# A hybrid decoder step on one core: one hand-made instruction list from the delta rule to the end

## The chip, the cores and the metric

The kernel runs on one core of a Trainium2 chip. The metric is the device time of one execution in microseconds (us), the median of the runs. Engines run their own queues in order and meet at semaphores: TensorE (PE in the profile; PEld is its weight load), VectorE (DVE), ScalarE (ACT), GpSimd (POOL) and SyncE (SP), which issues the DMAs.

## The reference, cut to what matters

One step of a decoder with two layers, for a prompt of 1024 tokens and 8 samples of one token, all in float32 with a model width of 1024.

```python
# layer A (gated delta rule), 8 heads of 128
proj = rmsnorm(x, norm_g) @ w_in                    # q, k, v, gate, a, beta
q, k, v = split(silu(causal_conv(proj[qkv])))       # then l2norm of q and k
o, s = gated_delta_rule(q, k, v, g, beta, s0)       # chunks, a state per head
h = x + (rmsnorm(o) * silu(gate)) @ w_out
# shared keys and values of 4 heads of 64
k, v = split(rmsnorm(h) @ w_kv); k = rmsnorm(k, k_norm)
# layer B (window of 128, ALiBi, sinks), 16 query heads in 4 groups
q, gate = split(rmsnorm(h) @ w_in); q = rmsnorm(q, q_norm)
o = softmax_with_sink(q k' - slope * dist) v
y = h + (o * silu(gate)) @ w_out
```

The states of the convolution and of the delta rule, and the last 128 keys and values, are outputs too, for the prompt and for the samples.

## The kernel before, in words

**Arithmetic.** Each operand of a large matrix product is split into a high part of the format fp32r and a low rest (`split`, line 79): ScalarE copies the high part, VectorE subtracts. A product is three chains of matmuls, high x high, high x low and low x high, added in one PSUM bank. The tokens are 8 tiles of 128, and a ninth "tile" (NT) for the 8 samples.

**The delta rule and the list.** From line 393 the program does not emit instructions directly. Generators yield operations (`Op`), and a planner, `Order` (line 478), keeps a planned clock for each engine and each piece of memory. It takes the operation that can start first by its plan (`run`, line 566), with a priority number as the tie-break, and emits it; the order so found is fixed for all engines (`tc.manual_schedule`, line 1388). A TensorE operation whose generator is no filler counts as ready `PEM` = 250 ns late, so filler matmuls go ahead of it. Durations come from formulas (`took`, line 442). The planner compares byte ranges inside a tile (`extent`, line 410; `ready`, line 509). `need` and `get` are waits of a generator for a named event or a free buffer, settled while the list is made; the semaphores between engines come from the framework behind it, which follows tiles and buffers.

Filler in this part is the first layer's input projection (`proj_all`, line 738) and, behind it, `out_all` (line 1363), the first 6 heads' share of the output projection (`K1` = 6): their results go through DRAM (`oD`) and come back in the order of tiles 0 to 7, two chains of 18 matmuls of 512 columns per tile. `out_evac` (line 1353) adds the input to it and stores each tile in DRAM (`hD`). The samples' delta rule comes in two batches of 4 heads (`sample_batch`, line 1147), behind head 3 and head 7; it loads 256 KB pieces of the state twice and stores them.

**Seam.** Behind the list the program closes the delta rule's buffers (line 1394) and is plain code from there on, whose order the framework finds. The loop over tiles at line 1407 loads each tile of `hD`, adds the last two heads' share (chains of 6 matmuls; `ohl`, line 1420, is its split operand; for the samples `ohs`, cleared on GpSimd by `zero_r`, line 1281, with 32 matmuls), stores it again, normalizes the rows, transposes them (line 1447) and splits them into `ng`, the operand of layer B.

**Layer B.** For each of 4 head groups `load_qkv` (line 1525) loads six pieces of weights of 256 KB, multiplies them by the norm's gain on GpSimd (line 92) and splits them. `tile_qkv` (line 1565) makes q, k and v of a tile, 24 matmuls of 384 columns into a bank `pj` (2 banks). Then it normalizes q per head, splits it (`qhl`), transposes the two parts (`tq`, line 1592, 4 transposes into bank `chA`), transposes k into the free columns of `pj`, makes scores with the high and low part of the keys (`sps`), the softmax, transposes of the probabilities (`ptp`, line 1645) and the product with the values (`op`, bank `chB`). The three stages of a tile are interleaved with those of its neighbours by `PIPE` (line 49). Gates (`gate_group`, line 1510: 24 matmuls of 384 or 264 columns into bank `ivY`) are put between by a table of positions (`gpos`, line 1673).

**Output projection.** From line 1702: the attention of the samples, which loads the key and value caches (`kc_`, `vc_`), and a projection in three column blocks with weights `wob`, 24 matmuls per tile, then `hD` is added and the result stored.

Of the kernel before, what the change touches and what calls it, by code (L numbers as in the profile page):

```python
# [20 lines left out]
P = 128  # L21
# [19 lines left out]
NY = 3  # L41
# [5 lines left out]
P3O = [0, 1, 2, 3, 8, 4, 5, 6, 7]  # L47

PIPE = [(1, 1), (0, 0), (2, 2)]
GA = 1  # L50
# [6 lines left out]
def hybrid_step(  # L57
# [384 lines left out]
    def took(op):  # L442
# [3 lines left out]
        name = op.f.__name__  # L446
        if op.e == "P":
# [17 lines left out]
        if op.e == "G":  # L465
            if name == "affine_select":
                return 130 + 1.25 * n
            if name == "tensor_tensor":
                return 100 + 2.35 * n
            return 100 + 0.8 * n if name == "memset" else 200 + 5 * n  # L470
# [7 lines left out]
    class Order:  # L478
# [45 lines left out]
        def emit(self, op, t_):  # L524
            c_ = took(op)
            self.at[op.e] = t_ + c_
            if op.e == "D":
                n = 1
                for d_ in (op.k["out"]).shape:
                    n *= d_  # L530
                self.dma = max(self.dma, t_) + n * 4 / 180.0
                end = self.dma + 2000.0
            else:
                end = t_ + c_ + AFTER[op.e]
# [573 lines left out]
    def store_state(h, st):  # L1108
        yield dq.dma_start(out=ssm_prompt[0, 0, h], in_=st)

# [36 lines left out]
    def sample_batch(h0):  # L1147


        B48 = [P, 4, NS]  # L1150
        units = [(hh, hb) for hh in range(4) for hb in range(2)]
# [10 lines left out]
        yield from need(*[("scb", nm, h0 + i) for nm in "qkv" for i in range(4)])  # L1162
        for u in units[:2]:
            yield load(*u)
        qs, ks, vs = (scb[:, i, h0:h0 + 4, :] for i in range(3))
        egs, bts = (smp[:, i, h0:h0 + 4, :] for i in range(2))
        t3 = gd.tile([P, 4, 4, NS], F32, tag="dl", name="t3", bufs=1)
# [5 lines left out]
        yield pm(sps[:, 0:96], ones, flat(t3[:, 0:3]))  # L1173
        sp = gd.tile([P, 4, 4, NS], F32, tag="dl", name="sp", bufs=1)
        yield sq.copy(flat(sp[:, 0:3]), sps[:, 0:96])
        free("gen")
        rs = sm.tile([P, 2, 4, NS], F32, tag="rs", name="rs", bufs=1)
        yield from rsq(vq, flat(rs), flat(sp[:, 0:2]), 64, 1.0, EPS,
# [4 lines left out]
        kq = sm.tile([P, 4, NS, 2], F32, tag="kq", name="kq", bufs=1)  # L1183
# [3 lines left out]
        spk = sm.tile([P, 4, NS, 2], F32, tag="spk", name="spk", bufs=1)  # L1187
        for i, (hh, hb) in enumerate(units):
# [6 lines left out]
            if i + 2 < 8:  # L1195
                yield load(*units[i + 2])
# [11 lines left out]
        yield vq.tensor_copy(st3[:, 0, :, 0:8], kn)  # L1208
        yield vq.tensor_copy(st3[:, 0, :, 8:16], st3[:, 0, :, 0:8].bitcast(F32))
        yield vq.tensor_tensor(out=st3[:, 0, :, 16:24], in0=kn, in1=st3[:, 0, :, 0:8].bitcast(F32), op=ALU.subtract)  # L1210
        yield vq.tensor_copy(st3[:, 1, :, 0:8], de)
        yield vq.tensor_copy(st3[:, 1, :, 16:24], st3[:, 1, :, 0:8].bitcast(F32))
        yield vq.tensor_tensor(out=st3[:, 1, :, 8:16], in0=de, in1=st3[:, 1, :, 0:8].bitcast(F32), op=ALU.subtract)
# [11 lines left out]
        yield pm(sps[:, 0:32], ones, o2.rearrange("p h b -> p (h b)"))  # L1225
        ro = kqn
        yield from rsq(vq, ro.rearrange("p h b -> p (h b)"), sps[:, 0:32], 32, 1.0 / 128.0, EPS,
# [3 lines left out]
        for hb in range(2):  # L1231
# [10 lines left out]
            for hh in range(4):  # L1242
                if hh < 3:
                    yield again(hh + 1)
# [8 lines left out]
        yield from need(*[("z", h0 + i, 2) for i in range(4)])  # L1253
        om = ogm[:, h0:h0 + 4, :]
# [26 lines left out]
    def zero_r(t_, scr):  # L1281
        G.memset(scr, 0.0)
        G.tensor_copy(t_, scr)
# [7 lines left out]
    def out_gains(p3a):  # L1291
# [7 lines left out]
        free("gen")  # L1299

    rawfree = [0] * RB[0]

    def out_loads():
# [3 lines left out]
        todo = [("w", 0, k, ts(0, 512)) for k in range(K1)] + [("o", 0, k) for k in range(0, K1, 3)]  # L1307
        todo += [("w", 1, k, ts(1, 512)) for k in range(K1)]
        for t in range(1, NT):
            todo += [("o", t, k) for k in range(0, K1, 3)]  # L1310
            if t in (2, 3):
                todo += [("w", 2, k, ts(t - 2, 512)) for k in range(K1, KT)]
        pieces = {}

        def feed2():
            yield from need(("split", 2 * len(jobs) - 1))
            for i, it in enumerate(todo):
                if it[0] == "o":
                    t, k = it[1:]
                    if k == 0:  # L1320
                        yield from need(("o", K1 - 1), ("out",))
                        if t >= 2:
                            yield from need(("ot", t - 2))
                        ohx[t] = (p3a[0].tile([P, D], F32, tag="hx", name="hx"),
                                  p3a[0].tile([P, 2, K1, P], F32R, tag="ohl", name="ohl"))
# [27 lines left out]
    def out_evac(t, ci, ps):  # L1353
# [3 lines left out]
        if ci:  # L1357
            yield dq.dma_start(out=hD[ts(t, P), :], in_=hx)
# [4 lines left out]
    def out_all():  # L1363
# [8 lines left out]
        for t in range(NT):  # L1372
# [8 lines left out]

    for i in range(2):
        for gi in range(4):
            mark("e", i, gi)
    for gi in range(3):
        mark("z", 0, gi)
    ET = mybir.EngineType
    with tc.manual_schedule(engines={ET.PE, ET.DVE, ET.Activation, ET.Pool, ET.SP}):
        for pri, gen_ in ((0, chains()), (1, inverses()), (2, prep_all()), (2.5, decays()), (3, values()), (2.2, norms()),
                          (5, conv_all()), (1.2, feed()), (1.2, split_all()), (7, samples()), (FILL, proj_all())):  # L1390
            spawn(pri, gen_)
        od.run()
    wb = wb_[0]
    es2.close()

    es4 = ExitStack()
    ng = []
    for i, (_, gn) in enumerate(GRP):
        npool = es4.enter_context(tc.tile_pool(name=f"npool{i}", reuse_waits="tile", bufs=1))
        ng.append(npool.tile([P, 2, KT, gn], F32R, name=f"ng{i}"))  # L1400
    hs = npool.tile([P, KT, 40], F32R, name="hs")
    with tc.tile_pool(name="p3", reuse_waits="tile", bufs=2) as p3:
        scr = p3.tile([P, KT, 40], F32, tag="scr", name="scr", bufs=1)
        zero_r(hs, scr)
        ohs = p3.tile([P, KT, 40], F32R, tag="ohs", name="ohs", bufs=1)
        zero_r(ohs, scr)
        for t in P3O:
            samp = t == NT
            n = NS if samp else P
            g, off = divmod(t * P, 384)  # L1410
            hx = p3.tile([P, D], F32, tag="hx", name="hx", bufs=4)
            DMA.dma_start(out=hx[:n], in_=x_sample[:, 0, :] if samp else hD[ts(t, P), :])
            if samp:
                S.copy(ohs[:, :, 0:NS], ogm)
                V.tensor_tensor(out=ohs[:, :, 32:32 + NS], in0=ogm, in1=ohs[:, :, 0:NS].bitcast(F32), op=ALU.subtract)
            else:
                ohl = p3.tile([P, 2, KT - K1, P], F32R, tag="ohl", name="ohl2")
                oc = ogs[:, :, ts(t, P)]
                S.copy(ohl[:, 0], oc)
                V.tensor_tensor(out=ohl[:, 1], in0=oc, in1=ohl[:, 0].bitcast(F32), op=ALU.subtract)  # L1420
            for ci in range(2):
                c_ = ts(ci, 512)
                ps = pj.tile([P, 512], F32, tag="pj", name="pj")
                if samp:
                    for b in range(2):
                        for k in range(KT):
                            w_ = wa[ci][:, b, k, :] if k < K1 else wb[:, b, k - K1, c_]
                            mm(ps[:40], ohs[:, k, :], w_, b + k == 0, b + k == KT)
                else:
                    for i, (a, b) in enumerate(PRS):  # L1430
                        for k in range(KT - K1):
                            mm(ps, ohl[:, a, k, :], wb[:, b, k, c_], i + k == 0, i == 2 and k == KT - K1 - 1)
                V.tensor_tensor(out=hx[:n, c_], in0=hx[:n, c_], in1=ps[:n], op=ALU.add)
                if samp:
                    V.tensor_tensor(out=hx[:n, c_], in0=hx[:n, c_], in1=ps[32:32 + n], op=ALU.add)
            DMA.dma_start(out=hD[t * P:t * P + n, :], in_=hx[:n])
            hn = p3.tile([P, D], F32, tag="hn", name="hn", bufs=3)
            ss = sm.tile([P, 1], F32, tag="ss", name="ss")
            r = sm.tile([P, 1], F32, tag="r1", name="r1")
            S.activation(hn[:n], hx[:n], AF.Square, accum_out=ss[:n])  # L1440
            rsqrt(r[:n], ss[:n], 1, 1.0 / D, EPS, n, tag="b")
            S.activation(hn[:n], hx[:n], AF.Copy, scale=r[:n])
            for hf in range(2):
                ps = gps("hps").rearrange("p (k t) -> p k t", k=4)
                k0 = 4 * hf
                for k in range(4):
                    PE.transpose(ps[:, k, :n], hn[:n, ts(k0 + k, P)], ident[:n, :n])
                hi = ng[g][:, 0, k0:k0 + 4, off:off + n]
                S.copy(hi, ps[:, :, :n])
                V.tensor_tensor(out=ng[g][:, 1, k0:k0 + 4, off:off + n], in0=ps[:, :, :n], in1=hi.bitcast(F32),  # L1450
                                op=ALU.subtract)
                if samp:
# [409 lines left out]
```

## Time and profile before

| | us |
|---|---|
| median of 3 runs (1298.38 to 1307.5) | 1305.35 |
| the profiled execution | 1303.65 |
| its span, first to last instruction | 1302.0 |
| TensorE busy | 1227.2 (94%) |
| TensorE weight loads busy | 1112.0 (85%) |
| VectorE busy | 926.3 (71%) |
| ScalarE busy | 634.8 (49%) |
| GpSimd busy | 288.4 (22%) |

The mean granted clock of TensorE is 0.986. A busy time is a share of the whole span; what ends a stretch is read from that stretch. A matmul's span is modelled and can hold short waits, so the distance from one start to the next says what a matmul costs.

### The profile page before, as it was taken

Reading aid. Unit: us, or ns where it says so; the run is one execution under the profiler, and the core shown is the slowest. Engines: PE = TensorE matmul, PEld = TensorE weight load, DVE = VectorE, ACT = ScalarE, POOL = GpSimd, SP = SyncE. Lnnn points to the kernel's source line nnn. Section 1 sums busy time; section 2 is a strip of 40 time slices with the busy share of each in tenths; the row PEclk is TensorE's granted clock in tenths of the full one; section 3 lists DMA queues with packets and bytes.
Section 4 is the critical chain, followed back from the end, with each engine's and each line's share of the span. In section 5 each row is a group of like instructions: output and inputs, shape, how many; then the busy total and the mean of one; then the engine's idle time right before and its main releaser. Section 6 shows DMA issues by size and latency. Waiting matters only on the chain.

```text
span 1302.0 us, 24333 instructions
## 1 busy us (share of the span) xinstructions
PE 1227.2 (94%) x8887; PEld 1112.0 (85%) x8887; DVE 926.3 (71%) x2656; ACT 634.8 (49%) x1812; POOL 288.4 (22%) x404
## 2 busy tenths in 40 slices
PE   4999999999999999998999978999989999999998
PEld 3989898989999989888988746888878888988897
DVE  7468988878979897788877358686675677677221
ACT  5236555645455553546453137375565556567100
POOL 1036423424324353253301122120030020000000
PEclk9999999999999999999999989999999999999999
DMA  7021111110221322111256666121030030102322
GB/s 239 1 81 35 36 33 36 37 51 18 68 66 35 98 67 84 36 36 31 61 176 195 200 220 176 34 59 26 1 82 3 1 82 20 33 2 88 117 91 73
DMA packets 131987, 92.03 MB, mean 71 GB/s; under 512 B 33880, under 2 KB 123712, under 8 KB 131808
## 3 DMA queue, kind: packets, MB, share of 16 engines
q1 hardware_dynamic: 131868, 90.48, 23.6%
q8 instruction: 70, 1.15, 0.4%
q14 instruction: 49, 0.40, 0.1%
HBM read 69.28 MB, written 23.25 MB: 71 GB/s over the span
## 4 chain that ended last, share of the span: by engine, by line
PE 70%; DVE 17%; ACT 4%; DMA 4%; issue 3%; POOL 2%; SPq 0%; DVEq 0%; ACTq 0%; POOLq 0%
PE pj L542 24%; PE pj L99 17%; PE ivt L542 4%; DVE co L542 3%; PE sps L99 3%; PE chB L542 3%; PE op L99 2%; PE chA L542 2%; PE ptp L1645 1%; DMA out_dram<-hx 1%; DVE wqkv L81 1%; PE sp L542 1%; PE nps L542 1%; PE tq L1592 1%; PE psab L99 1%
## 5 line engine op out<-in xcount | busy, mean ns | idle before, releaser
L542 PE MATMUL pj<-xg,whi 128*128 128x384 f32 (+1 forms) x1392 | 289.9, 335 | 1.0 <-ACT whi L542 1.0
L542 PEld LDWEIGHTS pj<-xg,whi 128*128 128x128 f32 x1392 | 222.6, 190 | 2.7 <-ACT whi L542 1.2
L99 PE MATMUL pj<-wqkv,ng 128*128 128x384 f32 x768 | 154.6, 346 | 0.0
L542 PE MATMUL pj<-xg,wlo 128*128 128x384 f32 (+1 forms) x696 | 151.9, 335 | 0.0
L542 DVE SCALAR_TENSOR_TENSOR co<-ue,cvT,co 128x528 f32<-128x528 f32 x144 | 134.6, 941 | 16.1 <-ACT co L542 14.5
L99 PEld LDWEIGHTS pj<-wqkv,ng 128*128 128x128 f32 x768 | 133.2, 191 | 5.0 <-issue 4.6
L542 PEld LDWEIGHTS pj<-xg,wlo 128*128 128x128 f32 x696 | 111.8, 189 | 1.4 <-issue 0.7
L92 POOL TENSOR_TENSOR raw<-raw,gains 128x512 f32<-128x512 f32 x40 | 45.8, 1154 | 255.5 <-DMA raw<-in_w_in_b_dram 147.1
L99 PE MATMUL pj<-wob,oh 128*128 128x384 f32 (+1 forms) x576 | 98.1, 325 | 0.0
L99 PEld LDWEIGHTS pj<-wob,oh 128*128 128x128 f32 x576 | 90.7, 191 | 1.8 <-issue 1.5
L542 PE MATMUL pj<-woa,ohl 128*128 128x512 f32 x288 | 76.1, 406 | 0.0
L542 PEld LDWEIGHTS pj<-woa,ohl 128*128 128x128 f32 x288 | 51.7, 188 | 11.6 <-issue 1.5
L542 ACT COPY ue<-pj 128x384 f32<-128x384 f32 (+1 forms) x88 | 31.7, 377 | 53.1 <-PE pj L542 46.1
L1823 DVE TENSOR_TENSOR hx<-hx,pj 128x384 f32<-128x384 f32 (+3 forms) x27 | 13.7, 508 | 60.5 <-PE pj L99 45.9
L542 POOL TENSOR_TENSOR ue<-ue,co 128x528 f32<-128x528 f32 x24 | 33.9, 1412 | 71.1 <-ACT ue L542 71.1
L542 DVE TENSOR_TENSOR wlo<-raw,whi 128x512 fp32r<-128x512 f32 x58 | 43.6, 758 | 7.7 <-ACT whi L542 7.6
L542 ACT ACTIVATE ue<-co 128x528 f32<-128x528 f32 x48 | 30.8, 644 | 29.9 <-DVE co L542 27.7
L542 ACT CAST whi<-raw 128x512 fp32r<-128x512 f32 x58 | 35.8, 619 | 16.8 <-PE pj L542 16.5
L542 POOL TENSOR_TENSOR co<-co,ue 128x528 f32<-128x528 f32 x24 | 39.3, 1636 | 1.3
L99 PE MATMUL op<-pt,vsb 128*64 128x256 f32 x240 | 37.9, 396 | 0.9 <-DVE e L1629 0.8
L1536 ACT ACTIVATE jk<-pj 128x320 f32<-128x320 f32 x32 | 13.9, 435 | 50.4 <-PE pj L99 50.4
L99 PE MATMUL pj<-woa,ohl 128*128 128x512 f32 x96 | 27.7, 442 | 11.2 <-DVE ohl L1420 5.8
(906 smaller groups left out, 2965.9 us busy)
## 6 DMA issues: line engine op xcount, KB each, us to landing
raw<-in_w_in_a_dram SPq DMA_DIRECT2D x64, 256.0 KB
ssm<-in_state_ssm_dram SPq DMA_DIRECT2D x32, 256.0 KB
hD<-hx SPq DMA_DIRECT2D x16, 512.0 KB
raw<-in_w_in_b_dram SPq DMA_DIRECT2D x32, 256.0 KB
xt<-in_x_prompt_dram SPq DMA_DIRECT2D x8, 512.0 KB
out_dram<-ssm SPq DMA_DIRECT2D x16, 256.0 KB
raw<-in_w_out_a_dram SPq DMA_DIRECT2D x16, 256.0 KB
hx<-in_x_prompt_dram SPq DMA_DIRECT2D x8, 512.0 KB
```

The lines of the kernel that those rows point to most:

```text
L81: V.tensor_tensor(out=lo, in0=raw, in1=hi.bitcast(F32), op=ALU.subtract)
L92: G.tensor_tensor(out=raw, in0=raw, in1=gain[:, k:k + n].unsqueeze(2).broadcast_to([P, n, c]), op=ALU.mult)
L99: PE.matmul(out, lhsT, rhs, start=start, stop=stop, skip_group_check=True)
L542: op.f(*op.a, **op.k)
L1536: S.activation(jk[:n], src, AF.Square)
L1592: PE.transpose(tq[:, ts(h, P)], qhl[:, h].rearrange("p a d -> p (a d)"), identr)
L1645: PE.transpose(pp[:, ts(h, P)], pr[h // 2][:, h % 2, ts(kt, P)], ident)
L1823: V.tensor_tensor(out=hx[:n, :cn], in0=hx[:n, :cn], in1=ps[:n, :cn], op=ALU.add)
```

## The change

- The planner's list goes on to the end of the program. All the plain code behind line 1394 becomes generators: `second`, `third`, `norms_b`, `scale_b`, `turns_b`, `w_feed`, `w_gain`, `w_split`, `qkv_all`, `gates`, `front`, `turn`, `mid`, `soft`, `back`, `outs`, `out_b`, `sample_attention`.
- The first 6 heads' output projection takes the tiles in the order 4, 5, 6, 7, 2, 3, 0, 1. Tiles 0 to 3 stay in SBUF and are not stored to `hD`; the last two heads' share of tiles 2, 3, 0 and 1 follows (`b_early`, `b_mms`) when the first half of head 7 is normalized. The sample tile and tiles 4 to 7 come behind.
- The samples' batches have 4, 3 and 1 heads, behind heads 3, 6 and 7.
- In layer B q is transposed before it is split, two fp32 transposes in place of four. They and the product with the values are two halves of one tile in bank `chA`; `chB` becomes a third bank for q, k and v and the output projection.
- Output tiles are taken in the order in which their operands are ready.

```diff
+    SB = {3: (0, 4), 6: (4, 3), 7: (7, 1)}
...
-            if h % 4 == 3:
-                yield from sample_batch(h - 3)
+            if h in SB:
+                yield from sample_batch(*SB[h])
...
+    AO = [4, 5, 6, 7, 2, 3, 0, 1]
...
-        for t in range(NT):
+        for t in AO:
             for ci in range(2):
...
+    BO = [2, 3, 0, 1, NT, 4, 5, 6, 7]
...
+    def b_mms(t):
+        yield from need(("bo", t))
+        ohl = bt_[t][1]
+        for ci in range(2):
+            yield from get("pj")
+            ps = pj.tile([P, 512], F32, tag="pj", name="pj")
+            if t == NT:
...
+            else:
+                for i, (a, b) in enumerate(PRS):
+                    for k in range(KT - K1):
+                        yield pm(ps, ohl[:, a, k, :], wb_[0][:, b, k, ts(ci, 512)], i + k == 0, i == 2 and k == KT - K1 - 1)
+            spawn(1.5, b_evac(t, ci, ps, NS if t == NT else P))
+        mark("bm", t)
+
+    def b_early():
+        yield from need(("out",), ("n", 2 * H - 2))
+        for i, t in enumerate(BO[:4]):
+            yield from need(("bm", BO[i - 2]) if i >= 2 else ("ot", AO[6 + i]))
+            yield from b_open(t, ohx[t][0], p3a[0], K1)
...
+    def second():
+        yield from need(("n", 2 * H - 1), ("smp",), ("gains",), *[("sts", h) for h in range(H)],
+                        *[("o", h) for h in range(K1)])
+        es2.close()
...
+        yield gq.memset(ohs.bitcast(F32), 0.0)
+        yield gq.memset(p4["hs"].bitcast(F32), 0.0)
...
+    def w_pieces():
+
+        for g in range(NKV):
+            yield ("wq", g), ("bm", NT) if g < 2 else ("qd", g - 2)
+            for m in (2 * g, 2 * g + 1):
+                yield ("gw", m), ("gm", m - 2, 2) if m >= 2 else ("p4",)
+        for ci in range(3):
+            yield ("wo", ci), ("qd", 2 + ci) if ci < 2 else ("wod", 0)
...
+        p4["sq"] = chp.tile([P, 512], F32, tag="chA", name="tqop")
...
+        pjbank.append("chB")
+        free("pj")
+        mark("p4")
...
+            tq = p4["sq"][:, 0:256].rearrange("p (j t) -> p j t", j=2)
+            for j in range(2):
+                yield pt(tq[:, j, :], qn[:, 2 * j:2 * j + 2].rearrange("p a d -> p (a d)"), ident)
+            yield from need(("kn", ti))
+            tk = ps[:, 384:512]
+            yield pt(tk, kn.rearrange("p a d -> p (a d)"), ident)
...
+            for e in range(2):
+                a_, b_ = slice(e * HD, e * HD + HD), slice(HD - e * HD, P - e * HD)
+                yield sq.copy(qse[a_, e], tq[a_])
+                yield vq.tensor_tensor(out=qse[b_, e], in0=tq[a_], in1=qse[a_, e].bitcast(F32), op=ALU.subtract)
...
+            op = p4["sq"][:, 256:512]
+            yield Op("P", op_block, (op, *vp), {})
...
+                          (1.3, b_early()), (1.4, norms_b()), (1.3, second()), (1.3, third()), (FILL, b_all()), (1.2, w_feed()), (1.2, w_gain()),
+                          (1.2, w_split()), (FILL + 1, qkv_all()), (FILL + 2, gates()), (2, front()), (1.8, turn()), (1, mid()), (0.5, soft()), (0, back()),
+                          (1.4, outs()), (FILL + 3, out_b()), (5, sample_attention())):
```

## Rows read from the trace of the kernel before

**Rows 1.** Stretches: length, busy PE PEld DVE ACT POOL (instructions), PEclk, DMA, GB/s.

```profile
97.65:651.00 553.35, 532.67 (x4567) 500.26 (x4567) 465.65 (x990) 291.66 (x872) 207.97 (x301) 0.99 0.17 49
...
749.00:814.00 65.00, 51.95 (x247) 36.90 (x246) 45.20 (x159) 35.26 (x61) 16.06 (x22) 0.92 0.63 198
944.00:976.00 32.00, 28.33 (x182) 25.30 (x181) 25.90 (x79) 20.10 (x57) 10.61 (x10) 0.95 0.34 83
976.00:1041.00 65.00, 65.00 (x409) 57.72 (x408) 41.88 (x193) 35.74 (x116) 0.79 (x1) 0.97 0.01 2
1205.00:1270.00 65.00, 63.39 (x386) 60.13 (x385) 13.86 (x36) 6.40 (x17) 0.00 (x0) 0.97 0.32 102
```

**Rows 2.** Waits of TensorE over the span: us in total, times, longest.

```profile
PE tq L1592 <- DVE qhl L1581: 6.6, 5, 2.9
...
PE pj L99 <- DVE ohl L1420: 5.8, 1, 5.8
...
PE pj L99 <- DVE hx L1433: 3.4, 1, 3.4
```

**Rows 3.** Timeline of VectorE at the seam: start, us, instruction, count, idle before and releaser.

```profile
755.88 0.69 DVE L542 TENSOR_TENSOR ssm<-ssm,up 128x512 f32<-128x512 f32 x1 [4.77 <-POOL ssm L542]
...
763.30 0.23 DVE L1415 TENSOR_TENSOR ohs<-ogm,ohs 128x64 fp32r<-128x64 f32 x1 [5.91 <-ACT ohs L1414]
...
767.44 0.15 DVE L121 TENSOR_SCALAR rs_x<-ss 128x1 f32<-128x1 f32 x1
```

**Rows 4.** Timeline of ScalarE at the seam.

```profile
763.03 0.24 ACT L1414 CAST ohs<-ogm 128x64 fp32r<-128x64 f32 x1 [24.70 <-POOL ohs L1283]
```

**Rows 5.** Chain of work that ended last: start, us, what, count.

```profile
885.92 2.46 PE gps__11116 L99 x13
...
982.66 2.46 PE gps__12292 L99 x13
...
1077.87 2.46 PE gps__13468 L99 x13
...
1205.32 6.76 DMA kc__14947<-in_cache_k_win_dram
...
1228.41 46.47 PE pj L99 x266
```

**Rows 6.** Timeline of TensorE within a head group of layer B.

```profile
984.98 0.53 PE L1592 MATMUL tq<-identr,qhl 128*128 128x128 f32 x4
985.35 0.41 PE L99 MATMUL gps__12292<-ng,gw 128*128 128x384 f32 x1
...
987.36 0.40 PE L99 MATMUL sps<-kTh,qst 128*128 128x256 f32 x2
...
988.49 2.44 PE L99 MATMUL pj<-wqkv,ng 128*128 128x384 f32 x13
990.77 0.38 PE L1645 MATMUL ptp<-ident,s__12162 128*128 128x128 f32 x2
...
991.56 1.99 PE L99 MATMUL pj<-wqkv,ng 128*128 128x384 f32 x10
993.55 1.08 PE L99 MATMUL op<-pt,vsb 128*64 128x256 f32 x8
994.56 0.61 PE L99 MATMUL pj<-wqkv,ng 128*128 128x384 f32 x2
```

**Rows 7.** Groups by line and shape, 815 to 1205: count, busy us, mean ns, idle before.

```profile
L1594 ACT CAST qst<-tq 128x512 fp32r<-128x512 f32 x32 | 18.5, 578 | 3.6 <-PE tq L1592 3.5
...
L1581 DVE TENSOR_TENSOR qhl<-qn,qhl 128x256 fp32r<-128x256 f32 x32 | 15.6, 487 | 3.8 <-ACT qhl L1580 3.4
...
L1580 ACT CAST qhl<-qn 128x256 fp32r<-128x256 f32 x32 | 12.8, 399 | 10.4 <-DVE qn L1577 9.7 <-DVE d L1635 0.7
```

**Rows 8.** Tile `sp` of the sample batches: durations in ns, first and last start.

```profile
L542 PE MATMUL sp<-t,ones x4: 247/275/322, 336.5 to 635.7; 128*128 128x96 f32 x4
```

**Rows 9.** Group of TensorE by line and shape: count, busy, mean, idle before.

```profile
L542 PE MATMUL chB<-rr,tf 128*128 128x128 f32 x112 | 22.6, 283 | 0.8 <-ACT qs L542 0.7
```

More of the change, by code (lines that the diff above doesn't have):

```diff
@@ L1380, in out_all, with b_open @@
                 spawn(1.5, out_evac(t, ci, ps))
+    es4, esp3, esat, esg, es5 = (ExitStack() for _ in range(5))
+    ng, ngp, hx2, bt_, p3_, p4 = [], [], {}, {}, [], {}
+    def b_open(t, hx, pool, nk):
+        ohl = pool.tile([P, 2, nk, P], F32R, tag="ohl", name="ohl2")[:, :, :KT - K1]
+        bt_[t] = (hx, ohl)
+        oc = ogs[:, :, ts(t, P)]
+        yield sq.copy(ohl[:, 0], oc)
+        yield vq.tensor_tensor(out=ohl[:, 1], in0=oc, in1=ohl[:, 0].bitcast(F32), op=ALU.subtract)
+        mark("bo", t)
@@ new lines, in w_gain, with w_split @@
+    def w_gain():
+        for n in range(p4["nw"]):
+            yield from need(("wr", n))
+            tok, pool, rv, w_, gain = wpc[n]
+            if gain is not None:
+                yield gq.tensor_tensor(out=rv, in0=rv, in1=gain.unsqueeze(2).broadcast_to(list(rv.shape)), op=ALU.mult)
+            mark("wg", n)
+    def w_split():
+        for n in range(p4["nw"]):
+            yield from need(("wg", n))
+            tok, pool, rv, w_, gain = wpc.pop(n)
+            yield sq.copy(w_[:, 0], rv)
+            yield vq.tensor_tensor(out=w_[:, 1], in0=rv, in1=w_[:, 0].bitcast(F32), op=ALU.subtract)
+            rawfree.append(pool)
+            free("raw")
+            if wpc.get(("end", tok)) == n:
+                mark(*tok)
@@ new lines, in hybrid_step, with bank, unbank, qkv_all @@
+    qps_ = {}
+    pjbank = ["pj", "pj"]
+    def bank():
+        tag = pjbank.pop(0)
+        return (chp if tag == "chB" else pj).tile([P, 512], F32, tag=tag, name="pj"), tag
+    def unbank(tag):
+        pjbank.append(tag)
+        free("pj")
+    def qkv_all():
+        for i, (g, t) in enumerate(seq):
+            if i % 9 == 0:
+                yield from need(("wq", g))
+            w_ = wt["wq", g]
+            yield from need(("ng", t))
+            yield from get("pj")
+            ps, tag = bank()
+            if t == NT:
+                for b in range(2):
+                    for k in range(KT):
+                        yield pm(ps[:40, :384], p4["hs"][:, k, :], w_[:, b, k, :], b + k == 0, b + k == KT)
+            else:
+                gi, off = divmod(t * P, 384)
+                for j, (a, b) in enumerate(PRS):
+                    for k in range(KT):
+                        yield pm(ps[:, :384], ng[gi][:, a, k, off:off + P], w_[:, b, k, :], j + k == 0, j == 2 and k == KT - 1)
+            qps_[i] = ps, tag
+            mark("qk", g, t)
+            if t == NT - 1:
+                mark("qd", g)
@@ new lines, in gates @@
+    def gates():
+        yield from need(("p4",))
+        for m, gi in gorder:
+            yield from need(("gw", m), *[("ng", t) for t in tiles_of(gi)])
+            w_ = wt["gw", m]
+            gn = GRP[gi][1]
+            yield from get("gb")
+            ps = ivp.tile([P, 512], F32, tag="ivY", name="gps_")
+            for j, (wp_, part) in enumerate(((0, 0), (1, 0), (0, 1))):
+                for k in range(KT):
+                    yield pm(ps[:, :gn], w_[:, wp_, k, :], ng[gi][:, part, k, :gn], j + k == 0, j == 2 and k == KT - 1)
+            mark("gm", m, gi)
+            spawn(-1, gate_out(m, gi, ps))
@@ L1401, in hybrid_step @@
[L1401 to L1452, printed above, removed]
-                    G.tensor_copy(hs[:, k0:k0 + 4, 0:NS], hi.bitcast(F32))
-                    G.tensor_copy(hs[:, k0:k0 + 4, 32:32 + NS], ng[g][:, 1, k0:k0 + 4, off:off + n].bitcast(F32))
@@ L1829, in hybrid_step @@
-    es5.close()
+    es5.close()
+    es4.close()
 _INS = ['x_prompt', 'x_sample', 'state_conv', 'state_ssm', 'cache_k_win', 'cache_v_win',
```

1042 lines of the change are left out of this document (634 added, 408 removed).

## The prediction

> **What bounds the kernel now.** I read the stretches of the span first. In the 553 us of the delta rule, which a list already orders, TensorE is busy for 532.67 us; only behind it, in the part that the change puts into the same list, are there holes [rows 1]. The largest lies at 749 to 814: 65 us with 51.95 us of TensorE work, at a granted clock of 0.92. The others are small: 3.67 us idle and 0.95 at 944 to 976, and 0.97 in the stretch behind it and in the output projection [rows 1]. The waits name the big ones: 5.8 us until VectorE had made `ohl`, 3.4 us until VectorE had emptied a projection bank [rows 2].
>
> Neither is VectorE's own doing. At 755.88 it makes the last sum of the second sample batch after 4.77 us of waiting, and `ohl`, the operand of the last two heads, stands behind it in its queue; at 763.30 it has waited 5.91 us for ScalarE [rows 3], which had waited 24.70 us for a clear of `ohs` on GpSimd [rows 4]. So the hole comes from fixed queues at the seam of two stages: late, unimportant sample work stands in front of what TensorE needs.
>
> The second place does not show as idle time. From 976 to 1041 TensorE is busy for 65.00 of 65 us [rows 1], which read plainly leaves nothing to gain. So I price one of the four head groups from the rows. A run of 266 matmuls of the output projection takes 46.47 us, 0.175 us each [rows 5]. A group has 192 such matmuls for q, k and v (33.5 us), 144 for the gates (25.2, taking the narrow ones at the same price, which is high) and 16 for the samples (2.8). One tile's attention takes, start to start [rows 6]: 0.37 us for the q transposes, 0.95 for the scores (1.13 less one matmul), 0.79 for the probability transposes, 1.01 for the values; 3.12 us, times 8 tiles 25.0. That is 86.5 us. The same gate of successive groups starts 96.75 and 95.21 us apart [rows 5]: 9 to 10 us per group, some 37 us over four groups, go to waits that look busy. The Trainium skill, "Perfetto Trace Analysis", Identifying the Most-Contended Engine, says that matmul busy time tells little and the share of weight loads more; by that rule 7.3 of the 65 us are free (57.72 us of loads [rows 1]), 11% against my 10%.
>
> **The change, part by part.** Sums go against the profiled execution: 1303.65 us, of which 1302.0 us are span. It lies 1.70 us under the median of 1305.35.
>
> *The seam, -13 us.* Tiles 2, 3, 0 and 1 of the last two heads' projection need only the first half of head 7, so they follow the first projection directly. Four tiles of two chains of six 512-column matmuls cover about 11 us, then the sample tile and tiles 4 to 7 follow. The sample tile no longer needs a GpSimd copy: both clears are one memset each. The 9.2 us of the two named waits go; with the rest of the idle time it is 13.05 us, and 0.08 of the clock over 65 us is 5.2 us more [rows 1, 2]. New here is that the first q, k and v weights wait for the sample tile, whose weights hold their buffer: six pieces through SP, GpSimd, ScalarE and VectorE. Behind the sample tile tiles 4 to 7 and 72 transposes stand as cover, about 19 us (48 matmuls of 0.23 us, by their columns from the 0.175, and 72 transposes of 0.1); if the load took longer, the group's first matmul would be late next. After that three banks of q, k and v must bridge the time until the p3 buffers are empty. Ends: 0 and 18 us; I take 13, the idle time without the clock. On SP, four stores of hD and two net loads of 512 KB go; they shared a transfer share of 0.63 [rows 1], so I cost them at nothing.
>
> *Head groups, -16 us.* One list places each attention step by its planned time, and a TensorE step counts as ready 250 ns late if there is filling work, so projections and gates go ahead of it. Weights are asked for a group ahead. What it takes back is surest at a change of group: 3.67 us idle plus 0.05 of 32 us and 0.03 of 65 us of clock [rows 1], 7.2 us; not all of that belongs to the change of group, so 5.3 for each of three. Ends: 0 and the 37 us above. I am near the idle rows, since many small waits are also in the list's own stretch: 20.68 us of idle time from 97.65 to 651 [rows 1].
>
> *q transposes, -4.6 us.* Four per tile (0.37 us [rows 6]) become two of plain fp32. Eight such transposes take 0.79 us [rows 6], so 0.20; 0.17 saved in each of 32 tiles is 5.4, less a little for narrower mixing. The splitting moves behind them: ScalarE had 399 + 578 ns, now two of about 399; VectorE has two subtractions of 487 ns instead of one [rows 7], 15.6 us more in all. It was busy for 41.88 of 65 us [rows 1], so this is hidden; the scores now wait for the second subtraction, with the next projection as cover. The 6.6 us that TensorE waited in front of them [rows 2] are counted under the groups.
>
> *Output projection, -3 us.* The key cache's load stands on the chain for 6.76 us [rows 5], but the stretch has only 1.6 us of idle time and 0.03 of clock, 2 us [rows 1]. Dynamic order of output tiles gives 3; ends 0 and 3.6.
>
> *Sample batches 4, 3, 1, +1 us.* The second batch began at 635.7 us [rows 8] and ended at 756 [rows 3]. Three of its heads now start one head earlier. One more batch is some 40 small VectorE steps of 0.15 us [rows 3], 6 us in a stage where VectorE is busy for 84% [rows 1]. Ends: 0 and 6. The sixteen SSM loads and their stores stay as many.
>
> *Shared PSUM bank, +5 us.* The q transposes and the value product now take two halves of one bank, `chA`; before they had different ones. In the trace, TensorE writing one part of `chB` waited 0.7 us for ScalarE's reading of another [rows 9], though that matmul does not use what was read. The planner compares byte ranges and does not know this wait. Ends: nothing, and the whole reading of the q half, two ScalarE copies and two subtractions, 2 x (399 + 487) = 1.77 us [rows 7] times 32, 57 us. I take 0.16 us per tile, nearest to the 0.7 us of rows 9. The Trainium skill, "PSUM — Partial Sum Buffer", PSUM bank collisions, asks for exactly such guards, by bank and quadrant and not by address; that speaks against this part of the change.
>
> Memsets that go to GpSimd, and row scales that alternate between GpSimd and ScalarE, cost nothing: GpSimd is busy for 0.79 of 65 us in the steady stretch [rows 1].
>
> Sum: -13 - 16 - 4.6 - 3 + 1 + 5 = -30.6 us: 1303.65 becomes 1273, and 1.7 us more against the median, 1275.
>
> **The rivals.**
> 1. *The small waits go too.* The 250 ns rule lets filling work pass every step that is late, so 30 of the 37 us come back, all of the seam (18) and no bank wait: -18 - 30 - 4.6 - 3.6 = -56, 1249. For it: at every moment of the groups there are projections or gates ready. Against: the list's own stretch keeps waits.
> 2. *The holes move.* The first weights, or the buffers of the attention, come later than the cover lasts, and the list's planned times miss the chip's by enough that small waits return elsewhere. Then the q transposes and half the seam remain, -4.6 - 6.5 + 1 = -10: 1295. That the change does nothing at the group changes is included here; that it does nothing at all is excluded, since the order at the seam is different.
> 3. *Slower: the shared bank decides.* The list emits the value product close behind the next tile's q transposes, and TensorE, strictly in order, stands still through the four readings, with projections and gates queued behind. Gains of 36 us without the bank term are used up at 36 / 32 = 1.1 us per tile; at 1.77 us [rows 7] it is 1304 - 36 + 57 = 1325. 1% slower begins at 1.5 us per tile. For it: the planner is blind to it, and every engine in between runs to a fixed list. Against: the reading took 0.7 us in all where this already happens [rows 9], and the two steps belong to different tiles with about 10 us between. The PSUM page's rule, if the waits follow it, is this rival's mechanism.
>
> **How the numbers follow.** Forecast 0.50 (own range 1258 to 1291), rival 1 0.18, rival 2 0.19, rival 3 0.13. I take 1% (13 us) as what a measurement of this kernel can tell from no change. Faster by over 1% (under 1292): 0.48 + 0.18 + 0.05 of rival 2, 0.71; within 1%: 0.16; slower: 0.13. The range 1247 to 1307 leaves out rival 3 but for a little of it and the lower half of rival 1.
>
> **What would show it.** Right: no idle stretch of TensorE over 2 us at the end of the first projection, with tiles 2, 3, 0 and 1 directly behind it; the clock at 1.00 across the group changes; the same gate 90 us apart instead of 96; sample batch over before 715 us. Wrong: a wait of TensorE for the first `wqkv` split; `tqop` waiting for VectorE or ScalarE by more than 0.5 us per tile; a longer delta rule. If the groups are 95 us apart without idle time, the gain was only in the seam, and the priced 10 us were no waits but the price of changing between kinds of matmul.

## The result, and the profile after

The changed kernel takes 1337.43 us (median, 1332.54 to 1338.18), the kernel before 1304.86 us beside it: a ratio of 1.0249, 95% interval 1.0204 to 1.0294. The forecast was 1275 us, with a range up to 1307. The profiled execution has a span of 1336.1 us against 1302.0, 34.1 us more.

One instruction sorts these 34.1 us by place: `kTh`, which ScalarE makes once for each of the 32 tiles of layer B, shortly before the tile's projection bank comes free. First its row before, then after (durations in ns; first and last start):

```profile
L1598 ACT ACTIVATE kTh<-pj,qgain x32: 361/368/382, 828.4 to 1189.8; 128x128 fp32r<-128x128 f32 x32
```

```profile
L546 ACT ACTIVATE kTh<-pj,qgain x32: 346/368/385, 831.5 to 1242.7; 128x128 fp32r<-128x128 f32 x32
```

Up to the first tile the change loses 3.1 us (828.4 to 831.5), where the seam should have gained 13. From the first to the last tile it loses 49.8 (361.4 us become 411.2), where the groups should have gained 16 and the transposes 4.6. Behind the last tile it gains 18.8 (112.2 become 93.4). That last gain is not a faster stage: of the 624 matmuls of the output projection 165 now stand before the last tile's `kTh`, and 62 did before the change, 36.0 us of work there in place of 14.4. So the loss of 49.8 us is in part work that was only moved. The rest shows as idle time of TensorE between first and last `kTh`: 45.5 us, and 9.1 before.

The stretches of [rows 1] after the change, and one of 300 us within the head groups (same columns):

```profile
97.65:651.00 553.35, 532.87 (x4650) 499.96 (x4648) 467.82 (x1004) 288.97 (x864) 205.16 (x298) 1.00 0.18 52
749.00:814.00 65.00, 52.63 (x259) 40.22 (x258) 42.30 (x114) 32.42 (x73) 27.83 (x22) 0.95 0.58 176
944.00:976.00 32.00, 29.12 (x174) 25.35 (x173) 24.00 (x105) 18.07 (x62) 0.00 (x0) 0.95 0.00 1
976.00:1041.00 65.00, 59.41 (x379) 53.36 (x378) 46.28 (x169) 34.37 (x103) 11.31 (x10) 0.97 0.18 43
...
814.00:1114.00 300.00, 268.24 (x1667) 238.50 (x1666) 215.66 (x811) 159.56 (x486) 34.23 (x49) 0.97 0.14 37
```

And that last stretch before the change:

```profile
814.00:1114.00 300.00, 289.66 (x1823) 258.79 (x1824) 213.08 (x849) 171.63 (x525) 34.05 (x30) 0.98 0.14 35
```

The stage that the list already ordered is unchanged (532.67 before, 532.87 us busy after), the seam too (51.95 before, 52.63 of 65 us after), but in the head groups TensorE has 156 matmuls fewer and stands for 32 us instead of 10. The waits of TensorE over the span, against [rows 2]:

```profile
PE pj L546 <- DVE hx L546: 13.2, 13, 1.9
PE pj L546 <- DVE kTl L546: 6.5, 4, 2.8
...
PE gps__13585 L546 <- DVE oT L546: 3.5, 1, 3.5
PE hps L546 <- POOL hn L546: 3.4, 2, 2.4
PE tqop L546 <- DVE qn L546: 3.3, 4, 1.4
PE gps__10386 L546 <- DVE oT L546: 2.7, 1, 2.7
...
PE pj L546 <- ACT wqkv L546: 1.6, 1, 1.6
...
PE pj L546 <- ACT ohl L546: 1.5, 1, 1.5
```

The largest named hole of the seam, 5.8 us for `ohl`, is down to 1.5, and the 6.6 us for `qhl` in the head groups are gone; but the waits for `hx`, 3.4 and 0.8 us at the seam before, are 6.1 us there now. Most of the new time is waits for a bank: `pj` is a projection that waits until VectorE has emptied one (`hx`, `kTl`), `gps` a gate that waits for the one gate bank (`oT`). Between first and last `kTh` gates wait for 20.8 us in all, in gaps over 0.2 us; before it was 0.5. First TensorE, then VectorE, at such a place, 1003 to 1014 us:

```profile
1002.89 0.44 PE L546 MATMUL tqop<-ident,qn 128*128 128x128 f32 x2 [0.47 <-DVE qn L546]
1003.08 0.60 PE L546 MATMUL gps__12391<-ng,gw 128*128 128x384 f32 x2
...
1003.60 1.66 PE L546 MATMUL gps__12391<-ng,gw 128*128 128x384 f32 x8
1007.89 1.01 PE L546 MATMUL gps__12465<-ng,gw 128*128 128x384 f32 x2 [2.63 <-DVE oT L546]
```

```profile
1003.83 0.49 DVE L546 TENSOR_REDUCE ss<-jk 128x5 f32<-128x320 f32 x1 [0.62 <-ACT jk L546]
...
1005.04 0.69 DVE L546 TENSOR_TENSOR wqkv<-raw,wqkv 128x512 fp32r<-128x512 f32 x1
1005.76 0.42 DVE L546 TENSOR_TENSOR qst<-tqop,qst 64x256 fp32r<-64x256 f32 x1
...
1007.29 0.55 DVE L546 SCALAR_TENSOR_TENSOR oT<-oT,gps__12391 128x384 f32<-128x384 f32 x1
...
1009.19 0.42 DVE L546 TENSOR_TENSOR qn<-pj,r 128x256 f32<-128x256 f32 x1
...
1013.25 0.47 DVE L546 SCALAR_TENSOR_TENSOR kn<-pj,r,kgbc 128x64 f32<-128x64 f32 x2
```

Two gates follow each other, so the second waits 2.63 us for the bank, and no projection can fill in, since all three projection banks are held; the next one starts at 1009.55 us. VectorE explains why: from the sum of squares of a tile (`ss`) to its `kn` it takes 9.4 us, because splits of weights and of the tile before, a gate and four score steps (for which it also waits 1.4 us) are put between steps that need 2.9 us when they stand together (`front_first`, below). I measured how long a bank is held as the time from the start of a tile's squares (`jk`, the first reading of its bank) to the start of its `kTh`, mean of 32 tiles: 8.62 us before, 14.08 after. From the first matmul of a tile to the end of its last split (`kTl`) it is 16.6 us before and 36.1 after. Of the 45.5 us of idle time above, 31.3 fall at moments when all three projection banks hold a tile of q, k and v.

### The profile page after: what moved, and what is told of

The parts are those of the page before. It is cut to its first block, busy times and chain, and to the rows that moved or that the text cites. A ratio compares the mean times of both kernels' runs of the same rounds, so it can differ in the third digit from the quotient of the medians.

```text
span 1336.1 us, 24282 instructions
## 1 busy us (share of the span) xinstructions
PE 1225.0 (92%) x8829; PEld 1108.4 (83%) x8829; DVE 958.9 (72%) x2690; ACT 633.3 (47%) x1836; POOL 301.1 (23%) x440
## 3 DMA queue, kind: packets, MB, share of 16 engines
q8 instruction: 70, 1.15, 0.4%
## 4 chain that ended last, share of the span: by engine, by line
PE 70%; DVE 18%; issue 3%; DMA 3%; ACT 3%; SPq 2%; POOL 1%; DVEq 0%; ACTq 0%; POOLq 0%
PE pj L546 39%; PE ivt L546 4%; PE sps L546 3%; DVE co L546 3%; PE chB L546 3%; PE pj L94 2%; PE tqop L1944 2%; PE chA L546 2%; DVE rs_u L546 2%; PE ptp L546 2%; SPq L546 2%; DMA hx<-hD 1%; DVE hx L546 1%; PE sp L546 1%; DVE oT L546 1%
## 5 line engine op out<-in xcount | busy, mean ns | idle before, releaser
L546 PE MATMUL pj<-woa,ohl 128*128 128x512 f32 x384 | 106.7, 415 | 8.4 <-DVE hx L546 5.3
L546 PE MATMUL pj<-wob,oh 128*128 128x384 f32 (+1 forms) x576 | 102.5, 332 | 8.7 <-DVE hx L546 4.7
L546 PEld LDWEIGHTS pj<-woa,ohl 128*128 128x128 f32 x384 | 69.1, 192 | 25.9 <-DVE hx L546 7.2
L546 DVE TENSOR_TENSOR hx<-hx,pj 128x512 f32<-128x512 f32 (+5 forms) x66 | 39.6, 602 | 60.8 <-PE pj L546 32.6
L546 DVE TENSOR_TENSOR wlo<-raw,whi 128x512 fp32r<-128x512 f32 x58 | 45.1, 782 | 12.4 <-ACT whi L546 12.2
L546 PE MATMUL sps<-kTh,qst 128*128 128x256 f32 (+1 forms) x144 | 41.1, 300 | 0.0
L546 DVE TENSOR_TENSOR qst<-tqop,qst 64x256 fp32r<-64x256 f32 x64 | 27.0, 422 | 19.4 <-ACT qst L546 13.7
L546 PE MATMUL sps<-kTl,qst 128*128 128x256 f32 (+1 forms) x144 | 38.4, 290 | 0.7 <-DVE kTl L546 0.7
```

The costliest lines, as they stand in the source:

```text
L546: op.f(*op.a, **op.k)
```

## The experiments

All are the changed kernel with an edit. Any edit lets the list order everything anew, so two of them only measure what such a new order changes by chance.

**Chance.** `nudge_245` and `nudge_255`:

```
-D0, PEM, VF, DP = 12000.0, 250.0, 1.0, 2000
+D0, PEM, VF, DP = 12000.0, 245.0, 1.0, 2000      # and 255.0
```

> The delay of 250 ns becomes 245, which means nothing in itself and only lets the list choose differently where two starts are close. Measures how much of any difference between lists is chance. If lists differ by chance by no more than 5 us, the time is 1332 to 1342 and hn_act's 12 us and sb44's 7 us are effects; if chance is 10 us or more, these two can't be told from it, and only the 22 us of the third bank, the 27 us of front_first and the 36 us of no_delay can.

> The same with 255 ns: a second draw of the same kind. Same bounds: 1332 to 1342 if chance is below 5 us.

Measured: 1344.20 and 1339.05 us, 6.8 and 1.6 over the changed kernel. Both draws came out slower. Differences under some 7 us between two lists say nothing of their edit. From first to last tile the two nudges take 410.3 and 411.4 us, the changed kernel 411.2, so in that stretch they moved next to nothing.

**The shared bank (rival 3), and the third projection bank.** `two_banks` leaves out the lines that make `chB` a third projection bank; `own_bank` does that too and gives `chB` to the value product:

```
-        pjbank.append("chB")
-        free("pj")
...
-            op = p4["sq"][:, 256:512]
+            op = op_[:, 0:256]        # op_: a tile of 512 columns in chB
```

> The value product gets the bank chB to itself, as before the change, and the projection keeps two banks instead of three. Shared-bank theory (the prediction's rival 3): the wait of TensorE for the readings of the q half goes, and the time falls by 13 to 57 us, to 1280 to 1324. Starved-list theory: in the head groups TensorE stands because projections and gates, its filling work, have no free bank while VectorE and ScalarE empty them in a fixed order; a bank less for the projection makes that worse, and the time rises by 15 to 35 us, to 1352 to 1372.

> The projection keeps two banks, the value product stays in the shared bank chA and chB lies idle. Starved-list theory: 20 to 40 us slower than the changed kernel, 1357 to 1377. The difference to the run with its own bank for the value product is the price of the shared bank alone: 30 us or more by the shared-bank theory, 0 to 6 us by the prediction's own figure of 0.16 us per tile (5 us).

Measured: 1359.02 us for `own_bank` and 1359.97 for `two_banks`. Between them lies 1 us, less than chance moves: the price of the shared bank can't be told from nothing, nor from the 5 us of the prediction; the 30 us or more of the shared-bank theory are excluded. The third projection bank is worth 22 us: TensorE lacks banks. In the profiled execution of `two_banks` 8.8 us of it lie between first and last tile and 10.2 behind, since the output projection uses the same banks.

**The q path.** In `q_no_sub` the low halves of q are left out, a clear by GpSimd stands in for each subtraction.

```
-  yield vq.tensor_tensor(out=qse[b_, e], in0=tq[a_], in1=qse[a_, e].bitcast(F32), op=ALU.subtract)
+  yield gq.memset(qse[b_, e].bitcast(F32), 0.0)
```

> Leaves out both subtractions that make the low halves of q (a clear by GpSimd stands in for each, so the low halves are zero): 64 VectorE instructions of 0.42 us, 27 us of VectorE in all, and the link ScalarE-VectorE-ScalarE in the split. If the changed q path is what slowed the groups: 15 to 30 us faster, 1307 to 1322. If VectorE's share is no bound and the list's order is: 0 to 6 us faster, 1331 to 1337.

Measured: 1343.92 us, no gain. A bank was held for 11.84 us, 2.2 less than in the changed kernel, so a shorter hold alone need not show in the time. The rows that answer to [rows 7] (groups, 800 to 1260 us) show the waits which tempted to the other theory:

```profile
L546 DVE TENSOR_TENSOR qst<-tqop,qst 64x256 fp32r<-64x256 f32 x64 | 27.0, 422 | 19.4 <-ACT qst L546 13.7 <-PE tqop L1944 4.2
L546 ACT CAST qst<-tqop 64x256 fp32r<-64x256 f32 x64 | 23.3, 364 | 15.5 <-DVE qst L546 7.2 <-PE tqop L546 5.9 <-DVE oT L546 1.5
```

The 4.2 us for `tqop` of line 1944 are the shared bank (VectorE waits for the value product, which writes the other half), the 13.7 and 7.2 the link between the engines; taking out the subtractions or the shared bank brought no time back that these runs could tell.

**GpSimd's row scales.** In `hn_act` ScalarE makes all nine.

```
-            if j % 2:
-                yield sq.activation(hn[:n], hx2[t][:n], AF.Copy, scale=p4["rn", t])
-            else:
-                yield gq.tensor_scalar_mul(hn[:n], hx2[t][:n], p4["rn", t])
+            yield sq.activation(hn[:n], hx2[t][:n], AF.Copy, scale=p4["rn", t])
```

> All nine row scales before the transposes of the second layer go to ScalarE (1.15 us each in the trace of after) instead of every second to GpSimd (2.85 to 3.12 us there, where the list reckons 1.48). If the seam's lost gain is GpSimd's: first gate 3 to 6 us earlier than 812.2 and the whole 3 to 8 us shorter, 1329 to 1334. If the seam is held by the projection banks and VectorE: first gate within 1.5 us of 812, the time within 3 us of 1337.

Measured: 1325.05 us, 12.4 less, and the first gate at 804.7 us instead of 812.2. The tile `hn` in the changed kernel:

```profile
L546 POOL TENSOR_SCALAR hn<-hx,rn x5: 2847/2853/3119, 762.6 to 811.6; 128x1024 f32<-128x1024 f32 x4, 8x1024 f32<-8x1024 f32 x1
L546 ACT ACTIVATE hn<-hx,rn x4: 1144/1149/1155, 762.6 to 801.9; 128x1024 f32<-128x1024 f32 x4
```

TensorE's transposes wait for GpSimd (3.4 us for `hn` above). From the end of the delta rule to the first gate it is 103.5 us in the changed kernel, 100.9 and 102.7 with the two nudges, 97.2 here; but 98.6 in `two_banks` and `own_bank`, which keep GpSimd's scales, so the first gate proves little. To the first `kTh` it is 122.8, with the nudges 122.4 and 122.0, and 118.7 here; on top of `front_first` (below) the same edit makes 119.2 of 122.7. So 3 to 4 us belong to this edit; the other 8 are about what chance moves.

**The order on VectorE and ScalarE.** `front_first` changes two priority numbers:

```
-  (2, front()), (1.8, turn()), (1, mid()), (0.5, soft())
+  (-0.1, front()), (-0.2, turn()), (1, mid()), (0.5, soft())
```

> Only two priorities change: the steps that empty a projection bank (statistics, scaling, transposes and splits of q and k) go before scores and softmax where both could start. Starved-list theory: the banks come back sooner, and a part of the 22 us that the third bank is worth (two_banks against after) is won again: 8 to 25 us faster, 1312 to 1329. If VectorE's total work were the limit, only the order on it would change: within 6 us of 1337.

Measured: 1309.89 us, 27.5 less, the largest gain of a single edit. A bank is held for 8.15 us, and TensorE is idle for 25.5 us between first and last `kTh` instead of 45.5. The same steps on VectorE, and the row of `kTh`:

```profile
1004.72 0.48 DVE L546 TENSOR_REDUCE ss<-jk 128x5 f32<-128x320 f32 x1
1005.24 0.23 DVE L546 TENSOR_SCALAR rs_x<-ss 128x5 f32<-128x5 f32 x1
...
1007.32 0.42 DVE L546 TENSOR_TENSOR qn<-pj,r 128x256 f32<-128x256 f32 x1
1007.66 0.47 DVE L546 SCALAR_TENSOR_TENSOR kn<-pj,r,kgbc 128x64 f32<-128x64 f32 x2
```

```profile
L546 ACT ACTIVATE kTh<-pj,qgain x32: 361/367/376, 830.1 to 1185.9; 128x128 fp32r<-128x128 f32 x32
```

From first to last tile it is 355.8 us, 55.4 less than in the changed kernel and 5.6 less than before. Behind the last tile it is 120.1 us instead of 93.4, since fewer holes are left that the output projection could fill: 48 of its matmuls stand before the last `kTh`, instead of 165.

**What the list does not know.** `taught` changes the planner alone: `ready` orders engines on one PSUM bank, each hand-over takes 60 ns more (a round number that I chose), and a chain of fp32r behind matmuls of another type starts 85 ns later. The last is in the trace: in the changed kernel, between first and last `kTh`, it is 259 ns from the start of such a chain's 384-column matmul to the next start behind probability transposes (33 cases), 176 behind scores, which are fp32r too (58 cases), and 174 behind its own kind (medians). The 60 ns are not: where an engine had waited, it started 32 to 55 ns after the end of what released it (medians by pair of VectorE, ScalarE and TensorE, whose ends are modelled), and the list already adds 70 behind VectorE and ScalarE. They are a margin, not a measured cost.

```
+  if BANK:                                  # in ready(): any part of a PSUM tile (PSN: their names)
+      for (tile_, *_x), write in op.use:
+          if tile_.name in PSN:
+              for w, rd in self.region(tile_, write).values():
+                  if w[0] != op.e: t_ = max(t_, w[1])
+                  for e, x in rd.items():
+                      if e != op.e: t_ = max(t_, x)
...
-  AFTER = {"P": 250.0, "V": 70.0, "S": 70.0, "G": 90.0}
+  AFTER = {"P": 310.0, "V": 130.0, "S": 130.0, "G": 150.0}
...
+  if kd and not self.kd: c_ += 85.0         # in emit(): kd is a matmul of fp32r, self.kd the last one's
```

> [...] No instruction is added. Wrong-times theory (the plan slips against the chip, and fixed queues then wait at the head): 10 to 30 us faster, 1307 to 1327, part of it in the delta rule. If the holes lie in the plan itself: within 6 us of 1337.

Measured: 1326.32 us, 11.1 less. The delta rule ended 9.2 us later (717.9 against 708.7), what follows was 21 us shorter (601.8 against 623.1 us until the last matmul of the output projection). A bank was held for 14.21 us, as long as in the changed kernel, so this gain has another cause than the holding time. So `tail_taught` has this knowledge for the part behind it only, from the first layer's output projection on (`if ("out",) in self.toks`), on top of `first_act`, which joins `front_first` and `hn_act`:

> front_first and hn_act together. They act in different stages (the seam until 814 us, the head groups behind it), so if both gains are what they seem, they add: 27 and 12 us off 1337, 1295 to 1301, under the kernel before (1302). If the gain of hn_act was only another order of the list by chance: 1304 to 1313.

> first_act with the taught costs (bank order, 60 ns more per hand-over, 85 ns at a change of type) from the first layer's output projection on, and nothing else. If the holes behind the delta rule come from a list that does not know the chip's waits: 10 to 25 us under first_act, 1282 to 1297, most of the way to tail_joined (1276.7). If they come from VectorE and ScalarE not being able to empty the banks faster: within 5 us of 1307.

Measured: 1307.23 us for `first_act`, so the gains did not add (2.7 us on top of `front_first`, within chance), and 1285.78 for `tail_taught`, ratio to before 0.9878 (0.9836 to 0.9920): 21 us by the three taught costs alone. Which of the three brings them was not separated. Its stretch of head groups and its `kTh`:

```profile
814.00:1114.00 300.00, 283.07 (x1831) 251.76 (x1831) 240.34 (x948) 174.17 (x555) 25.40 (x24) 1.00 0.12 30
```

```profile
L564 ACT ACTIVATE kTh<-pj,qgain x32: 358/368/375, 826.5 to 1156.4; 128x128 fp32r<-128x128 f32 x32
```

The same tile of successive groups (the fifth) comes 89.5, 89.3 and 89.8 us apart; before 95.0, 95.5 and 93.1, in the changed kernel 100.9, 100.6 and 106.6. With 1831 matmuls in the same 300 us and VectorE busier than before (240.34 against 213.08 us), capacity of the engines was not the limit.

**The 250 ns delay.** `no_delay` sets it to 0.

> Only the 250 ns by which a TensorE step with filling work beside it counts as late are set to 0, in the whole list. The prediction took this delay for what lets filling work pass late steps and brings 16 us back. If it does: 10 us or more slower, 1347 and up. If filling work is missing for want of banks and not of rank: within 8 us of 1337 in the part behind the delta rule; the rule itself, which the same number orders, may end some us earlier or later.

Measured: 1373.12 us, 36 more, 27 of them in the delta rule (its end at 735.3) and 9 behind it. The delay matters, but mostly where it was before the change.

**Sample batches, gates, and all together.** `sb44` has batches of 4 and 4 heads; `first_act_gates` lets gates go ahead of projections, held to their tile's place:

```
-    SB = {3: (0, 4), 6: (4, 3), 7: (7, 1)}
+    SB = {3: (0, 4), 7: (4, 4)}                                # sb44
...
+            gp_ = 8 * (m // 2) + 3 * gi - 3 + m % 2            # first_act_gates, in gates()
+            if gp_ - 2 >= 0:
+                yield from need(("tr", gp_ - 2))
...
-  (FILL + 2, gates())
+  (FILL - 0.5, gates())
```

> Sample batches of 4 and 4 heads again, all else as changed. The prediction gave three batches 1 us (0 to 6). If that stands: 0 to 6 us faster, 1331 to 1337, with the last clear between the projections later by some us since the second batch ends later. If the early batch took VectorE's time in the delta rule, the rule ends 3 to 6 us before 708.7 and the whole is 6 to 15 us shorter.

> As first_act, and gates go ahead of projections but not before their place in the order of tiles. Gates-as-filling theory (gates one behind the other wait for their one bank, about 2 us each time, in after at 811 to 1150 us): 5 to 15 us faster than first_act. If the holes are not at the gates: within 5 us of first_act or slower, since a projection is then missing where a gate stands.

Measured: 1330.22 us for `sb44`, 7 less and at the edge of chance, with the rule's end at 702.2 against 706.1 to 712.7 in the nudges and the original. 1314.89 for `first_act_gates`, 7.7 more than `first_act`. There no gate waits any more between first and last `kTh` (5.8 us in `first_act`), but the projections of q, k and v wait for 16.8 us instead of 8.5 (gaps over 0.2 us): the waits only moved to the other banks, so gates one behind the other are a symptom. A second bank for gates was not tried. Both edits entered a joined version. `joined` is `taught`, `first_act_gates` and `no_delay` with 8 value buffers (`vsb`) in place of 4; `tail_joined` adds `sb44` and has the taught costs and the missing delay only from the first layer's output projection on:

> Taught costs, no 250 ns delay before TensorE's steps, the emptying steps first, all row scales on ScalarE, gates ahead of projections but held to their place in the order of tiles, value buffer of 8 tiles. If the holes are made by the list's order and by GpSimd's scaling, as the runs so far say, these add up to 35 to 65 us: 1272 to 1302, under the kernel before. If the list cannot do without them because VectorE and ScalarE simply take the time: 1310 to 1330.

> joined, but with the taught costs and without the 250 ns delay only from the output projection of the first layer on, and with sample batches of 4 and 4 heads. In joined and taught the delta rule ended 10 us later than in after (718 against 708.7 us), in sb44 6.5 us earlier (702.2), and the stretch behind it was shorter. If these parts add up: 1295 less 10 to 17, 1278 to 1285. If the delta rule's gain is lost again at the seam: 1285 to 1295.

Measured: 1295.04 us, ratio 0.9940 (0.9921 to 0.9958), and 1276.70, ratio 0.9826 (0.9795 to 0.9858), the fastest of all. Which of its four further parts makes the 9 us between it and `tail_taught`, little more than chance moves, was not separated. Its row of the head groups:

```profile
814.00:1114.00 300.00, 291.53 (x1901) 263.51 (x1900) 244.17 (x947) 179.22 (x556) 27.54 (x41) 0.99 0.13 34
```

## Why the prediction was wrong

**Head groups, -16: the step that failed.** The price of a group stood the test: 86.5 us of TensorE work, and 89.5 us per group where a list does it well. That it fits so well is partly luck: it took 48 narrow gate matmuls some 2.6 us too dear (an estimate by their columns from the 0.175 us) and left out some 2.3 us for the dearer first matmul of a chain behind matmuls of another type (98 cases before the change between first and last `kTh`, by kind 73 to 108 ns in the median). What failed is the sentence that the list lets projections and gates go ahead of late steps. Filling work needs a bank, and I took "at every moment there are projections or gates ready" from the counts of matmuls, without asking how long a bank is held. The hand-written order of before held one for 8.62 us; the list, which gave statistics, scaling and splits of q and k the last rank among the attention steps on VectorE and ScalarE, for 14.08. Put in front by two numbers, 27 us return: that is the cause for most of the loss. A further 21 return when three costs are added to the list's plan. This is not the holding time (8.06 us in `first_act`, 7.83 in `tail_taught`). I had named the list's blindness for one bank only; that late steps in a fixed order make all behind them late fits the gain, but which cost mattered stays open.

**Seam, -13.** It came out at +3.1 to the first tile. The early tiles did what I said, the projection of q, k and v began at 787.7 us instead of 808.1, but other work was late in turn: the evacuation of projection banks (6.1 of the 13.2 us for `hx`) and GpSimd's scales. I had costed these scales at nothing because GpSimd was idle. Idle it was, but TensorE's transposes wait for the result, and it takes 2.85 us against 1.15 on ScalarE; with ScalarE alone the first tile comes 3 to 4 us sooner. The sum of idle time at 749 to 814 us is nearly what it was, 12.4 us after 13.05; what else the gain was lost to was not traced.

**q transposes, -4.6.** TensorE's part was right: two transposes from 1002.89 to 1003.08, 0.19 us against my 0.20. VectorE's second subtraction was hidden, as said (`q_no_sub`).

**Output projection, -3.** No gain of its own could be seen; its tiles filled holes, and new waits for `hx` came (6.0 us behind 1190 us). Whether the two buffers of `hx5` make these was not tried.

**Sample batches, +1.** The last batch was not over before 715 us: its last product begins at 750.0 us, before the change at 749.7. By `sb44` alone the cost lies between nothing and 7 us.

**Shared bank, +5.** Measured 1, within chance, so small as I took it or smaller. The end at 57 and rival 3 fall: the slower side came, by another mechanism than the one named for it. The waits of VectorE for the other half of the bank are there, 4.2 us, and cost no time that the runs could tell. The Trainium skill, "PSUM — Partial Sum Buffer", PSUM bank collisions, asks for such guards; the trace agrees that they are kept.

Nearest was rival 2, holes that move because the planned times miss the chip's, but it kept half of the seam and lost nothing elsewhere. None of my cases let the hand-written order be better than the list, which is where the time in the head groups went.

**The signs that I had named.** Of those for right, one came: at the end of the first projection no idle stretch is over 2 us. The same tile of successive groups came 101 to 107 us apart and not 90, and the clock over the head groups was 0.97, before 0.98. Of those for wrong, the first q, k and v chain did wait for its weights, 1.6 us (`wqkv` above); the value products and q transposes (`tqop`) waited for 0.2 us per tile, less than the 0.5 named; the delta rule ended at 708.7 us, before at 708.1.

## What to carry to other kernels

Before counting on filling work, count what it needs: the banks, how long each is held from first matmul to last reading, and how many there are. In a list that places work by earliest start, the steps that give a scarce buffer back need the better rank, even over steps on the longest chain; a hand-written order can have this without saying so, and the profile shows it as the time from a bank's first reading to its last. That time is a sign and not the whole cause: here one edit shortened it by 2.2 us without gain, and another gained 11 us without shortening it. And where every edit makes a new order, nudge a meaningless number first: here two nudges moved the time by up to 7 us.

## What the hardware showed

VectorE's small steps stretch beside GpSimd. In `front_first`, VectorE, and under it GpSimd at the same time:

```profile
877.02 0.17 DVE L546 SCALAR_TENSOR_TENSOR r<-rs_u,r 128x5 f32<-128x5 f32 x1
877.22 0.92 DVE L546 TENSOR_TENSOR rs_u<-rs_x,r 128x5 f32<-128x5 f32 x1
878.17 0.17 DVE L546 TENSOR_TENSOR rs_u<-rs_u,r 128x5 f32<-128x5 f32 x1
878.38 0.93 DVE L546 SCALAR_TENSOR_TENSOR rs_u<-rs_u 128x5 f32<-128x5 f32 x1
```

```profile
877.08 4.20 POOL L546 TENSOR_TENSOR raw<-raw,gains 128x512 f32<-128x512 f32 x4 [44.84 <-DVE rs_u L546]
```

A step of 5 columns takes 0.92 us in place of 0.17 while GpSimd multiplies a weight piece (1.04 us each). Read one by one, each stretched step ends 0.02 us after one of these pieces, so it waits for the piece's end; the short step at 878.17 starts between two pieces. The Trainium skill, "SBUF — State Buffer", Who interferes with whom, says that a VectorE instruction with two SBUF inputs contends with a GpSimd instruction that reads SBUF; the rows agree. It is no cause of the difference here: what steps beside a GpSimd instruction took over the median of their kind, summed where it was over 0.15 us, is some 77 us before and 73 after.
